# A hybrid decoder layer: first feed-forward pair without block sums, shared raw buffers, operands moved to multiples of 256 bytes

## The chip, the cores and the metric

The kernel runs on one core of one Trainium2 chip. The metric is the device time of one launch in microseconds (us); lower is better. Five engines matter: TensorE (PE, matrix products into PSUM; PEld is its weight load), VectorE (DVE), ScalarE (ACT), GpSimd (POOL) and SyncE (SP), which issues most of the loads. Each engine works off its own queue in a fixed order.

## The reference, cut to what matters

One decoder layer on 1024 tokens of width 1024: a mixer of sparse attention and retention, and then the feed-forward part, which is all that the change touches.

```python
h = h + mix @ w_out[l]                      # 1024 tokens x 1024
hn = rms_norm(h, ln2_w[l])                  # h * rsqrt(mean(h*h) + EPS) * weight
h = h + jnp.square(jax.nn.relu(hn @ w_up[l])) @ w_down[l]   # 1024 -> 4096 -> 1024
```

## The kernel before, in words

All matrices are float32. A product is made of float32r pieces: each operand is split into a rounded high part (a cast on ScalarE, line 1003) and the rest (a subtraction on VectorE, line 174), and high x high, high x low and low x high are added up: three matmuls of 128x128 weights by 512 columns for one block of products.

`h` lies transposed in the tiles `hac0` to `hac7`, 128 features each, 1024 tokens in two halves. When the last row of the output projection is added to a tile (line 945), `scaled` stores the sum to the DRAM tensor `dH` through the POOL queue and multiplies it by the norm's weight. The norm's factor itself is put on later, since relu squared commutes with a positive factor: `v2` and `r2` are made from the squares of `h` (function `scale`), and `add` applies them.

The up projection goes by 16 pairs of weight tiles (`NU`). A pair is a 2x2 block product (two weight tiles by two halves of features, two halves of tokens), done by a scheme that takes 7 block products instead of 8 and pays with sums: of the weights (`sums_up`: S1 to S4), of `h` (`early_sums`, `late_sums`: T1 to T4, made once) and of the results. A block product is 4 feature tiles x 3 matmuls = 12 matmuls, so a pair has 84. Products are named by their weight operand: 11, 12, S2, S1, S3, S4, 22. The bank `px` collects 11, then S2, S3 and 22 on top, and between two of them ScalarE copies an intermediate value out (lines 1114 and 1122), so the next product waits for that copy.

`fetch_up` loads a pair's weights in four tiles of 256 KB (`small`, four buffers), `first_up` splits 11 and 12, `rest_up` the five others, each into one of 12 operand slots: 8 are the former `hac` tiles, on the left side of the memory, 4 (`wo8` to `wo11`) lie in the pool `fw` on the right side. The pools on the right side start below the small constants, at a remainder of 224 bytes to the next multiple of 256; the left side is at multiples of 256. The results are relu'd, squared and stored to `dU` (line 1108).

`scale` runs after pair 6 and after pair 8, for half the tokens each: eight loads of `h` into the buffers `tmp`, which the intermediate results use too, eight squares on ScalarE, seven adds on VectorE, a product with ones and a reciprocal.

The down projection takes the 32 tiles of `dU` and of `w_down` in 8 groups of four, split into `fd` (and `ma`) tiles, through four raw buffers that are allocated when the up phase has released its pools. Each group has 192 matmuls.

The order on each engine is not the program's: a scheduler places the instructions by a timeline of its own, and the queues then keep that order. Pools hand out buffers by tags; a new tile waits until the buffer's last user is done.

Of the kernel before, what the change touches and what calls it, by code (L numbers as in the profile page):

```python
# [101 lines left out]
def hybrid_layer(ctx, tc, xT, x, wfm, wv, vecs, pe, w1, w2, w_out, w_up, w_down,  # L102
# [48 lines left out]
    r1 = cst.tile([128, NT], F32, name="r1")  # L151
# [798 lines left out]
    def early():  # L950
# [4 lines left out]
        r2.extend(hs.tile([128, 512], F32, name=f"r2{hf}") for hf in range(2))  # L955
# [36 lines left out]
    NU, NG, CH = 16, 8, 4  # L992
    ups = ExitStack()
# [18 lines left out]
    def small(nm):  # L1012
        return fw.tile([128, 512], F32, name=nm, tag="w" + nm[0], bufs=4)
# [10 lines left out]
    def early_sums(m):  # L1024
        t2 = op.tile([128, 512], F32, name=f"t2{m}", tag="t2", bufs=2)
        minus(quarter(0, m, 0), quarter(0, m, 1), quarter(0, m, 0))
        minus(t2, quarter(1, m, 1), quarter(0, m, 0))
        split(part("T2", m), t2)
        minus(quarter(1, m, 0), quarter(1, m, 0), t2)

    def late_sums():
        for m in range(4):
            split(part("T1", m), quarter(0, m, 0))
        yield
# [3 lines left out]
        yield  # L1038
        for m in range(4):
            split(part("22", m), quarter(1, m, 1))  # L1040
        yield
        for m in range(4):
            split(part("T4", m), quarter(1, m, 0))
        yield
# [3 lines left out]
    def operand(p, n):  # L1048

        i = next(slots)  # L1050
# [12 lines left out]
    def first_up(p):  # L1063
        wu[p] = {}
        for i, n in enumerate(("11", "12")):
            wu[p][n] = operand(p, n)
            split(wu[p][n], wr[p][i])

    def sums_up(p):

        a1, a2, b1, b2 = wr[p]
        s1, s2, s3, s4 = (small(f"s{p}{i}") for i in range(4))
        minus(s1, b1, b2, ALU.add)
        minus(s2, s1, a1)
        minus(s3, a1, b1)
        minus(s4, a2, s2)
        wr[p] = s2, s1, s3, s4, b2

    def rest_up(p):

        for n, t in zip(("S2", "S1", "S3", "S4", "22"), wr.pop(p)):
            wu[p][n] = operand(p, n)
            split(wu[p][n], t)
            yield
# [3 lines left out]
    def up(p):  # L1088
# [20 lines left out]

        x = px.tile([128, 512], F32, name=f"px{p}")  # L1110
# [26 lines left out]

    fetch_up(0)
# [4 lines left out]
    sums_up(0)  # L1143
    pacc = Ring("A4")

    def ready(o, hf):
        scaled(o, 1)
        if o >= 4:
            early_sums(o - 4)
# [6 lines left out]
    for n in ("T1", "T3", "22", "T4"):  # L1156
        hhi[n] = [hq.tile([128, 512], F32R, name=f"bh{n}{m}") for m in range(4)]
        hlo[n] = [hq.tile([128, 512], F32R, name=f"bl{n}{m}") for m in range(4)]

    v2 = {}  # L1160

    def scale(hf):

        for o in range(NK):
            h = fp.tile([128, 512], F32, name=f"hs{o}{hf}", tag="tmp", bufs=6)
            nc.sync.dma_start(h, dH[o][:, 512 * hf:512 * hf + 512])
            if o == 0:
                nc.scalar.activation(r2[hf], h, AF.Square)
            else:
                nc.scalar.activation(h, h, AF.Square)  # L1170
                nc.vector.tensor_tensor(r2[hf], r2[hf], h, op=ALU.add)
        ps = pz.tile([128, 512], F32, name=f"pr{hf}")
        nc.tensor.matmul(ps, ones, r2[hf], start=True, stop=True)
        v2[hf] = fp.tile([128, 512], F32, name=f"rv2{hf}", bufs=1)
        nc.vector.tensor_scalar(v2[hf], ps, scalar1=1.0 / D, scalar2=EPS, op0=ALU.mult, op1=ALU.add)
        nc.vector.reciprocal(r2[hf], v2[hf])

    fetch_up(1)
    first_up(1)
    first = [up(0), up(1)]  # L1180
    for u in first:
        next(u)
    for _ in alternate(rest_up(0), late_sums()):
        pass
    sums_up(1)
    for _ in rest_up(1):
        pass
    fetch_up(2)
    for _ in first[0]:
        pass  # L1190
    first_up(2)
    for _ in first[1]:
        pass
    for p in range(2, NU):
        sums_up(p)
        for _ in rest_up(p):
            pass
        if p + 1 < NU:
            fetch_up(p + 1)
# [168 lines left out]
```

## Time and profile before

| | us |
|---|---|
| median of 3 runs (lowest, highest) | 1359.34 (1353.59, 1360.81) |
| profiled execution, its own time | 1358.02 |
| its span, first to last instruction | 1356.3 |
| PE busy | 1289.7 (95%) |
| DVE, ACT busy | 834.5 (62%), 610.2 (45%) |
| mean granted TensorE clock | 0.982 of full speed |

A busy PE is not a PE at its peak: its matmuls overlap, so their lengths (0.39 us) add up to more than the time they take. What counts is the distance from one start to the next, about 0.23 us for 512 columns, and the idle times between. Where the granted clock falls to half, the distance is 0.43 us.

### The profile page before, as it was taken

Reading aid. Unit: us, or ns where it says so; the run is one execution under the profiler, and the core shown is the slowest. Engines: PE = TensorE matmul, PEld = TensorE weight load, DVE = VectorE, ACT = ScalarE, POOL = GpSimd, SP = SyncE. Lnnn points to the kernel's source line nnn. Section 1 sums busy time; section 2 is a strip of 40 time slices with the busy share of each in tenths; the row PEclk is TensorE's granted clock in tenths of the full one; section 3 lists DMA queues with packets and bytes.
Section 4 is the critical chain, followed back from the end, with each engine's and each line's share of the span. In section 5 each row is a group of like instructions: output and inputs, shape, how many; then the busy total and the mean of one; then the engine's idle time right before and its main releaser. Section 6 shows DMA issues by size and latency. Waiting matters only on the chain.

```text
span 1356.3 us, 19627 instructions
## 1 busy us (share of the span) xinstructions
PE 1289.7 (95%) x6862; PEld 1100.9 (81%) x6862; DVE 834.5 (62%) x1920; ACT 610.2 (45%) x1225; POOL 320.4 (24%) x464
## 2 busy tenths in 40 slices
PE   8999998999999998899699998899989999999998
PEld 6888877999999887778488776688768888888886
DVE  7695774777788974777973545644357255434522
ACT  7333314577787773455664545454444022201200
POOL 0453335455565661121000110010100000000013
PEclk9999999999999999899899998899989999999999
DMA  6567398122222517921243333332386033213102
GB/s 231 160 207 218 111 275 267 59 87 87 79 75 79 214 55 206 253 93 56 72 152 101 117 127 115 132 125 86 112 301 216 31 124 125 78 47 124 62 31 93
DMA packets 82770, 175.73 MB, mean 130 GB/s; under 512 B 10944, under 2 KB 27712, under 8 KB 82672
## 3 DMA queue, kind: packets, MB, share of 16 engines
q1 hardware_dynamic: 68256, 127.51, 31.4%
q0 software_dynamic: 14416, 46.97, 9.0%
q8 instruction: 54, 0.88, 0.3%
q14 instruction: 44, 0.36, 0.1%
HBM read 123.91 MB, written 50.46 MB: 129 GB/s over the span
## 4 chain that ended last, share of the span: by engine, by line
PE 38%; issue 17%; DMA 4%; POOL 2%; DVE 1%; ACT 1%; POOLq 0%; SPq 0%; ACTq 0%; DVEq 0%
PE pd L1229 9%; PE pd L1231 9%; PE pd L1230 9%; DMA rg<-dRG 2%; PE px L1097 2%; PE px L1099 2%; PE px L1098 2%; POOL dU L1108 1%; PE py L1099 1%; PE py L1097 1%; PE py L1098 1%; DMA dMix<-m 1%; DMA mixa<-dMix 0%; DMA dwr<-in_w_down 0%; PE pz L1097 0%
## 5 line engine op out<-in xcount | busy, mean ns | idle before, releaser
L1229 PE MATMUL pd<-du,dw 128*128 128x512 f32 x512 | 198.4, 393 | 5.6 <-ACT dw L1003 5.6
L1230 PE MATMUL pd<-du,dw 128*128 128x512 f32 x512 | 199.3, 389 | 0.0
L1231 PE MATMUL pd<-du,dw 128*128 128x512 f32 x512 | 198.8, 389 | 0.0
L1238 DVE TENSOR_TENSOR y<-pd,y 128x512 f32<-128x512 f32 x128 | 87.4, 689 | 167.3 <-PE pd L1231 167.3
L1003 ACT CAST du<-dur 128x1024 fp32r<-128x1024 f32 x32 | 33.7, 1052 | 199.9 <-PE pd L1230 175.2
L1229 PEld LDWEIGHTS pd<-du,dw 128*128 128x128 f32 x512 | 97.1, 190 | 26.2 <-ACT dw L1003 6.0
L1230 PEld LDWEIGHTS pd<-du,dw 128*128 128x128 f32 x512 | 96.2, 188 | 20.2
L1231 PEld LDWEIGHTS pd<-du,dw 128*128 128x128 f32 x512 | 96.2, 188 | 19.9
L1108 POOL DMA_DIRECT2D dU<-u x64 | 34.7, 542 | 312.7 <-ACT u L1107 312.7
L1240 POOL TENSOR_TENSOR y<-y,r 128x512 f32<-128x512 f32 x14 | 18.1, 1295 | 331.9 <-DVE y L1238 331.9
L174 DVE TENSOR_TENSOR tl<-pt,th 128x512 fp32r<-128x512 f32 (+2 forms) x136 | 80.1, 597 | 14.7 <-ACT th L783 14.0
L783 ACT CAST th<-pt 128x512 fp32r<-128x512 f32 (+2 forms) x136 | 68.1, 515 | 22.5 <-PE pt L838 20.1
L1097 PE MATMUL px<-bhT,wS 128*128 128x512 f32 x128 | 55.1, 430 | 20.7 <-ACT s L1114 12.3
L838 PE MATMUL pt<-ident,p 128*128 128x128 f32 x456 | 71.8, 275 | 0.8 <-DVE sbias L706 0.5
L830 PE MATMUL po<-tl,v 128*128 128x256 f32 (+1 forms) x272 | 70.2, 293 | 0.8 <-DVE tl L174 0.8
L830 PE MATMUL po<-th,v 128*128 128x256 f32 (+1 forms) x272 | 68.7, 274 | 0.1
L774 POOL TENSOR_SCALAR p<-p,rs 128x896 f32<-128x896 f32 (+3 forms) x64 | 47.8, 747 | 48.3 <-DVE rs L772 20.4
L174 DVE TENSOR_TENSOR w<-raw,w 128x512 fp32r<-128x512 f32 x48 | 32.9, 690 | 40.0 <-ACT w L1003 39.1
L838 PEld LDWEIGHTS pt<-ident,p 128*128 128x128 f32 x456 | 52.4, 141 | 5.0 <-DVE tl L174 1.4
L1003 ACT CAST wS<-s 128x512 fp32r<-128x512 f32 x64 | 39.6, 618 | 36.9 <-PE px L1099 22.4
L758 ACT ACTIVATE p<-p,mn 128x896 f32<-128x896 f32 (+3 forms) x64 | 49.8, 778 | 13.7 <-DVE mn L751 13.0
L830 PEld LDWEIGHTS po<-tl,v 128*128 128x128 f32 x272 | 51.6, 190 | 2.1 <-DVE tl L174 1.4
(426 smaller groups left out, 3726.5 us busy)
## 6 DMA issues: line engine op xcount, KB each, us to landing
raw<-in_w_up SPq DMA_DIRECT2D x64, 256.0 KB, 3.1
dU<-u POOLq DMA_DIRECT2D x64, 256.0 KB, 2.7
dur<-dU SPq DMA_DIRECT2D x32, 512.0 KB, 4.6
dwr<-in_w_down SPq DMA_DIRECT2D x32, 512.0 KB, 4.6
xraw<-in_xT SPq DMA_DIRECT2D x16, 256.0 KB, 5.4
w1r<-in_w SPq DMA_DIRECT2D x32, 128.0 KB, 3.6
dQ<-stg_Q POOLq DMA_DIRECT2D x8, 512.0 KB, 5.3
q<-dQ SPq DMA_DIRECT2D x64, 64.0 KB, 2.4
```

Source lines behind the costliest of these rows:

```text
L174: eng.tensor_tensor(lo, src, hi.bitcast(F32), op=ALU.subtract)
L758: nc.scalar.activation(buf[:, :n], buf[:, :n], AF.Exp, scale=-1.0, bias=mn[:, u, fin:fin + 1], accum_out=sm[:, 0, u, 0:1])
L783: nc.scalar.copy(th[:, :w], pt[:, :w])
L830: mm = nc.tensor.matmul(po[:, cs], vals[g, kt // 4][:, kt % 4, br], q[:, o:o + 128 * len(us)], start=False, stop=end and q is parts[1])
L838: nc.tensor.transpose(pt[:, o:o + 128], res[u][0][:, c:c + 128], ident)
L1003: nc.scalar.copy(to[0], raw)
L1097: nc.tensor.matmul(ps, wh[:, cs], bh, start=first and m == 0, stop=False, skip_group_check=not first)
L1108: nc.gpsimd.dma_start(dU[2 * p + i][:, 512 * hf:512 * hf + 512], u)
L1229: nc.tensor.matmul(ps, wh[:, cs], uh[:, ts], start=i == 0, stop=False)
L1230: nc.tensor.matmul(ps, wl[:, cs], uh[:, ts], start=False, stop=False)
L1231: nc.tensor.matmul(ps, wh[:, cs], ul[:, ts], start=False, stop=i == CH - 1)
L1238: nc.vector.tensor_tensor(y, ps, y, op=ALU.add)
```

## The change

- Pair 0 is computed as the plain 2x2 product: 8 block products, no sums of weights or results. Its `h` operands 12 and 22 are split as soon as `h` is ready; the sums T1 to T4 of `h` are formed after it and first used by pair 1. T3 takes the buffers of 12.
- All raw loads, of the weights up, of `h` for the squares and of both down operands, go through one pool `raws` of three buffers of 512 KB, which stays for both phases. `sums_up` forms its sums in place, in the raw tiles.
- The squares of `h` are taken over whole tiles, one tile after each pair from 4 on (`norm`), instead of eight half tiles at once after pairs 6 and 8.
- The last pair uses only the 8 left slots, and the `fd` tiles are laid out so that the first group's lie where buffers become free first.
- `r1` is padded by 56 floats, which moves every right-side pool to a multiple of 256 bytes.

```diff
-    r1 = cst.tile([128, NT], F32, name="r1")
+    r1 = cst.tile([128, NT + 56], F32, name="r1")[:, :NT]
@@
-        r2.extend(hs.tile([128, 512], F32, name=f"r2{hf}") for hf in range(2))
+        r2.append(hs.tile([128, S], F32, name="r2"))
@@
+    raws = ctx.enter_context(tc.tile_pool(name="raws", side="right", reuse_waits="tile", bufs=3))
@@
-    def small(nm):
-        return fw.tile([128, 512], F32, name=nm, tag="w" + nm[0], bufs=4)
+    def raw_tile(nm):
+        return raws.tile([128, S], F32, name=nm, tag="raw")
@@ operand
-        i = next(slots)
+        i = next(j for j in slots if j < 8 or p < NU - 1)
@@ fetch_up
-            wr[p] = [small(f"raw{p}{i}") for i in range(4)]
+            wr[p] = [raw_tile(f"raw{p}{i}") for i in range(2)]
             for i, t in enumerate(wr[p]):
-                nc.sync.dma_start(t, w_up[2 * p + i // 2][:, 4 * (i % 2):4 * (i % 2) + 4].rearrange("p k c -> p (k c)"))
+                nc.sync.dma_start(t, w_up[2 * p + i].rearrange("p k c -> p (k c)"))
@@ sums_up
+        a1, a2, b1, b2 = blocks(p)
+        s1 = fw.tile([128, 512], F32, name=f"s{p}", tag="s", bufs=2)
+        minus(s1, b1, b2, ALU.add)
+        minus(b1, a1, b1)
+        minus(a1, s1, a1)
+        minus(a2, a2, a1)
+        del wr[p]
+        for n, t in (("S2", a1), ("S1", s1), ("S3", b1), ("S4", a2), ("22", b2)):
+            wu[p][n] = operand(p, n)
+            split(wu[p][n], t)
@@ up
+        if p == 0:
+            for hf, pair in ((0, ("11", "21")), (1, ("12", "22"))):
+                for i, ring in enumerate((px, py_)):
+                    ps = ring.tile([128, 512], F32, name=f"pp{hf}{i}")
+                    for j in range(2):
+                        product(ps, f"{i + 1}{j + 1}", pair[j], j == 0)
+                    relu2(ps, i, hf)
+                yield
+            return
@@ ready
-        if o >= 4:
-            early_sums(o - 4)
+        split(part("22" if o >= 4 else "12", o % 4), quarter(o // 4, o % 4, 1))
@@
-    def scale(hf):
+    def norm():
         for o in range(NK):
-            h = fp.tile([128, 512], F32, name=f"hs{o}{hf}", tag="tmp", bufs=6)
-            nc.sync.dma_start(h, dH[o][:, 512 * hf:512 * hf + 512])
+            h = raw_tile(f"hs{o}")
+            nc.sync.dma_start(h, dH[o])
...
+            yield
@@
+    for _ in up(0):
+        pass
+    fetch_up(1)
+    first_up(1)
+    for m in range(4):
+        early_sums(m)
+    both(hr, "T3", "12")
+    late_sums()
+    sums = norm()
+    for p in range(1, NU):
+        fetch_up(p + 1)
+        sums_up(p)
+        for _ in up(p):
+            pass
+        first_up(p + 1)
+        if p >= 4:
+            next(sums, None)
@@ down
+            pool, tag = (ma, f"m{2 * i + j}") if odd and n == 3 else (fd, f"d{odd}{n}{i}{j}")
+        firsts = [(0, 2, *x) for x in ij]
+        homes = {k: home(*k) for k in [(g, n, *x) for g, n in ((1, 0), (1, 1), (1, 2), (0, 3)) for x in ij]
+                 + firsts[:2] + [(0, n, *x) for n in (0, 1) for x in ij] + firsts[2:]}
@@
-                    raw = fd.tile([128, S], F32, name=f"d{nm}r{f}", tag="raw", bufs=4)
+                    raw = raw_tile(f"d{nm}r{f}")
```

Up to the start of the feed-forward part the order on every engine stays as it was. Three places behind it follow; the numbers at the names are buffer numbers.

VectorE where pair 0 begins, before: `s00` to `s03` are sums of weights, `t20` and `t21` parts of T2, `w11_0` is the low part of the first operand.

```order
L174 TENSOR_TENSOR w11_0_8462<-raw00_8422,w11_0_8462 128x512
L174 TENSOR_TENSOR w12_0_8465<-raw01_8423,w12_0_8465 128x512
L945 TENSOR_TENSOR hac3_6135<-ob311_8572,hac3_6135 128x512
L1007 TENSOR_TENSOR s01_8469<-s00_8468,raw00_8422 128x512
L1007 TENSOR_TENSOR s02_8470<-raw00_8422,raw02_8424 128x512
L1007 TENSOR_TENSOR hac0_6008<-hac0_6008 128x512
L945 TENSOR_TENSOR hac7_6243<-ob711_8585,hac7_6243 128x512
L1007 TENSOR_TENSOR hac1_6055<-hac1_6055 128x512
L1007 TENSOR_TENSOR hac2_6098<-hac2_6098 128x512
L1007 TENSOR_TENSOR s03_8471<-raw01_8423,s01_8469 128x512
L1007 TENSOR_TENSOR t20_8502<-hac4_6160,hac0_6008 128x512
```

The same place now: all four weight operands of pair 0, and then `bl12`, `bl22` (low parts of the `h` operands 12 and 22) among the first differences for T1.

```order
L175 TENSOR_TENSOR w11_0_8479<-raw00_8443,w11_0_8479 128x512
L175 TENSOR_TENSOR w12_0_8482<-raw00_8443,w12_0_8482 128x512
L175 TENSOR_TENSOR w21_0_8485<-raw01_8444,w21_0_8485 128x512
L175 TENSOR_TENSOR w22_0_8488<-raw01_8444,w22_0_8488 128x512
L946 TENSOR_TENSOR hac3_6134<-ob311_8581,hac3_6134 128x512
L1009 TENSOR_TENSOR hac0_6007<-hac0_6007 128x512
L175 TENSOR_TENSOR bl120_8431<-hac0_6007,bh120_8427 128x512
L946 TENSOR_TENSOR hac7_6242<-ob711_8596,hac7_6242 128x512
L175 TENSOR_TENSOR bl220_8439<-hac4_6159,bh220_8435 128x512
L1009 TENSOR_TENSOR hac1_6054<-hac1_6054 128x512
L175 TENSOR_TENSOR bl121_8432<-hac1_6054,bh121_8428 128x512
```

The sums of weights are gone from this place, and what only pair 1 needs stands behind what pair 0 needs.

ScalarE in the middle of the up phase, before: `hs` are tiles of `h` for the squares, `s17` is the copy that product S2 of pair 7 waits for.

```order
L1107 ACTIVATE u106_9711<-u106_9711 128x512
L1168 ACTIVATE r20_6000<-hs00_9715 128x512
L1170 ACTIVATE hs10_9718<-hs10_9718 128x512
L1003 CAST wS4_9_10102<-s93_10088 128x512
L1170 ACTIVATE hs20_9722<-hs20_9722 128x512
L1170 ACTIVATE hs30_9726<-hs30_9726 128x512
L1170 ACTIVATE hs40_9730<-hs40_9730 128x512
L1114 COPY s17_9802<-px7_9788 128x512
L1170 ACTIVATE hs50_9734<-hs50_9734 128x512
```

ScalarE at the corresponding place now, one tile of `h` in a pair's round: `s27` is the copy that product S3 of pair 7 waits for, `raw90` and `raw100` are weights of pairs 9 and 10.

```order
L1120 COPY s17_9722<-px7_9708 128x512
L1005 CAST wS3_8_9845<-raw81_9685 128x512
L1104 ACTIVATE u106_9670<-u106_9670 128x512
L1103 ACTIVATE u007_9737<-s17_9722 128x512
L1104 ACTIVATE u007_9737<-u007_9737 128x512
L1181 ACTIVATE hs4_9972<-hs4_9972 128x1024
L1128 COPY s27_9754<-px7_9708 128x512
L1131 COPY s57_9768<-py7_9741 128x512
L1005 CAST w11_9_9966<-raw90_9830 128x512
L1005 CAST wS4_9_9994<-raw90_9830 128x512
L1005 CAST w12_10_10115<-raw100_9976 128x512
L1005 CAST wS2_9_9985<-raw90_9830 128x512
```

The copy `s17` now stands ahead of the square, and `s27` right behind it.

ScalarE at the passage from the up to the down phase now (before, the order was the same but for the last square, which stood ahead of the first cast): `u1015` is the last result of the up phase, `d0000` and `d0010` the first operands of the down phase.

```order
L1103 ACTIVATE u0115_10962<-s215_10916 128x512
L1104 ACTIVATE u0115_10962<-u0115_10962 128x512
L1103 ACTIVATE u1015_10978<-px15_10870 128x512
L1005 CAST d0000_11007<-dur0_11017 128x1024
L1005 CAST d0010_11009<-dwr0_11021 128x1024
L1005 CAST d0100_11011<-dur1_11025 128x1024
L1104 ACTIVATE u1015_10978<-u1015_10978 128x512
L1005 CAST d0110_11013<-dwr1_11029 128x1024
```

The first casts of the down phase stand behind the relu of the last bank of the up phase.

## Rows read from the trace of the kernel before

**Rows 1.** Windows: busy us (count) of PE, PEld, DVE, ACT, POOL; clock; DMA.

```profile
641.90:708.50 66.60, 54.44 (x215) 42.25 (x214) 57.54 (x96) 41.98 (x74) 6.72 (x13) 0.92 0.33 114
708.50:995.10 286.60, 273.42 (x1145) 217.92 (x1144) 137.62 (x202) 143.72 (x254) 30.08 (x56) 0.98 0.36 118
...
1000.60:1350.80 350.20, 350.16 (x1536) 289.55 (x1536) 160.38 (x193) 63.31 (x62) 18.13 (x14) 0.99 0.31 106
```

**Rows 2.** Waits of PE from 590 us on: total us, times, longest.

```profile
PE px L1097 <- ACT s L1114: 12.3, 4, 5.0
PE px L1097 <- ACT s L1122: 8.4, 4, 6.3
PE pd L1229 <- ACT dw L1003: 5.6, 1, 5.6
```

**Rows 3.** Timeline, PE: start, us, line, tiles, [idle before, releaser].

```profile
645.80 0.50 PE L1099 MATMUL px<-bh,w 128*128 128x512 f32 x1 [0.68 <-DVE w L174]
...
675.82 0.80 PE L1097 MATMUL px<-bhT,wS 128*128 128x512 f32 x1 [6.34 <-ACT s L1122]
...
817.54 0.80 PE L1097 MATMUL px<-bhT,wS 128*128 128x512 f32 x1 [4.90 <-ACT s L1114]
...
818.13 0.63 PE L1098 MATMUL px<-blT,wS 128*128 128x512 f32 x1
...
818.56 0.63 PE L1099 MATMUL px<-bhT,wS 128*128 128x512 f32 x1
...
1000.64 3.78 PE L1229 MATMUL pd<-du,dw 128*128 128x512 f32 x8 [5.59 <-ACT dw L1003]
1004.22 0.52 PE L1230 MATMUL pd<-du,dw 128*128 128x512 f32 x1
```

**Rows 4.** Timeline, VectorE and ScalarE where they work without a pause.

```profile
645.07 1.28 DVE L174 TENSOR_TENSOR w<-raw,w 128x512 fp32r<-128x512 f32 x2
...
667.76 2.19 ACT L1003 CAST bh<-hac 128x512 fp32r<-128x512 f32 x4
```

**Rows 5.** Timeline, PE: the 204th matmul of the up phase.

```profile
708.55 0.40 PE L1099 MATMUL px<-bhT,w 128*128 128x512 f32 x1
```

**Rows 6.** Timeline, ScalarE: the first square of the first `scale`.

```profile
812.90 0.63 ACT L1168 ACTIVATE r<-hs 128x512 f32<-128x512 f32 x1 [1.62 <-DMA hs<-dH]
```

**Rows 7.** Timeline, PE: first of 12 matmuls, first behind them; pairs 2, 3, down.

```profile
724.98 0.39 PE L1097 MATMUL py<-bh,wS 128*128 128x512 f32 x1
...
727.70 0.39 PE L1097 MATMUL px<-bh,w 128*128 128x512 f32 x1
...
744.64 0.40 PE L1097 MATMUL py<-bh,wS 128*128 128x512 f32 x1
...
747.44 0.40 PE L1097 MATMUL px<-bh,w 128*128 128x512 f32 x1
...
1100.48 0.39 PE L1229 MATMUL pd<-du,dw 128*128 128x512 f32 x1
...
1103.20 0.39 PE L1229 MATMUL pd<-du,dw 128*128 128x512 f32 x1
```

**Rows 8.** DMA issues: queue, count, KB each, median us to landing.

```profile
raw<-in_w_up SPq DMA_DIRECT2D x64, 256.0 KB, 3.1
...
dur<-dU SPq DMA_DIRECT2D x32, 512.0 KB, 4.6
...
rv<-dRV SPq DMA_DIRECT2D x8, 512.0 KB, 6.3
```

**Rows 9.** The tile `y`, loads of `dH` of 512 KB, window 940 to 990 us.

```profile
DMA to landing us min/median/max: 3.4/3.6/4.2
```

**Rows 10.** Groups, VectorE: add of 1024 elements; busy us, mean ns.

```profile
L236 DVE TENSOR_TENSOR xacc<-xacc,xsq 128x1024 f32<-128x1024 f32 x7 | 8.5, 1218 | 0.2 <-ACT xsq L234 0.2
```

**Rows 11.** Timeline, ScalarE at the passage to the down phase.

```profile
995.48 0.58 ACT L1106 ACTIVATE u<-px 128x512 f32<-128x512 f32 x1
...
999.55 1.04 ACT L1003 CAST dw<-dwr 128x1024 fp32r<-128x1024 f32 x1 [0.76 <-DMA dwr<-in_w_down]
```

More of the change, by code (lines that the diff above doesn't have):

```diff
@@ L1024, in early_sums @@
     def early_sums(m):
-        t2 = op.tile([128, 512], F32, name=f"t2{m}", tag="t2", bufs=2)
+        t2 = fw.tile([128, 512], F32, name=f"t2{m}", tag="s", bufs=2)
         minus(quarter(0, m, 0), quarter(0, m, 1), quarter(0, m, 0))
@@ L1136, in up, with both @@
         yield
+    hr = ups.enter_context(tc.tile_pool(name="hr", side="right", reuse_waits="tile", bufs=1))
+    def both(pool, n, tag):
+        hhi[n] = [pool.tile([128, 512], F32R, name=f"bh{n}{m}", tag=f"h{tag}{m}") for m in range(4)]
+        hlo[n] = [pool.tile([128, 512], F32R, name=f"bl{n}{m}", tag=f"l{tag}{m}") for m in range(4)]
+    for n in ("12", "22"):
+        both(hr, n, n)
     fetch_up(0)
@@ L1155, in hybrid_layer @@
     hq = ups.enter_context(tc.tile_pool(name="hq", side="right", reuse_waits="tile", bufs=1))
-    for n in ("T1", "T3", "22", "T4"):
-        hhi[n] = [hq.tile([128, 512], F32R, name=f"bh{n}{m}") for m in range(4)]
-        hlo[n] = [hq.tile([128, 512], F32R, name=f"bl{n}{m}") for m in range(4)]
+    for n in ("T1", "T4"):
+        both(hq, n, n)
     v2 = {}
-    def scale(hf):
+    def norm():
         for o in range(NK):
-            h = fp.tile([128, 512], F32, name=f"hs{o}{hf}", tag="tmp", bufs=6)
-            nc.sync.dma_start(h, dH[o][:, 512 * hf:512 * hf + 512])
+            h = raw_tile(f"hs{o}")
+            nc.sync.dma_start(h, dH[o])
@@ L1167, in scale @@
             if o == 0:
-                nc.scalar.activation(r2[hf], h, AF.Square)
+                nc.scalar.activation(r2[0], h, AF.Square)
             else:
                 nc.scalar.activation(h, h, AF.Square)
[L1171 to L1175, printed above, removed]
@@ L1176, in scale @@
-        nc.vector.reciprocal(r2[hf], v2[hf])
+                nc.vector.tensor_tensor(r2[0], r2[0], h, op=ALU.add)
+            yield
+        for hf in range(2):
+            r = r2[0][:, 512 * hf:512 * hf + 512]
+            ps = pz.tile([128, 512], F32, name=f"pr{hf}")
+            nc.tensor.matmul(ps, ones, r, start=True, stop=True)
+            v2[hf] = fp.tile([128, 512], F32, name=f"rv2{hf}", bufs=1)
+            nc.vector.tensor_scalar(v2[hf], ps, scalar1=1.0 / D, scalar2=EPS, op0=ALU.mult, op1=ALU.add)
+            nc.vector.reciprocal(r, v2[hf])
+            yield
@@ L1178, in hybrid_layer @@
+    for _ in up(0):
+        pass
     fetch_up(1)
     first_up(1)
[L1180 to L1194, printed above, removed]
-        sums_up(p)
[L1196 to L1199, printed above, removed]
-            first_up(p + 1)
+    for m in range(4):
+        early_sums(m)
@@ L1209, in hybrid_layer, with home @@
         pd = Ring("D8")
-        places = [[(fd, f"d{g}{i}") for i in range(12 + 4 * g)] + [(ma, f"m{k}") for k in range(4 - 4 * g)] for g in range(2)]
+        def home(g, n, i, j):
+            odd = g % 2
+            pool, tag = (ma, f"m{2 * i + j}") if odd and n == 3 else (fd, f"d{odd}{n}{i}{j}")
+            return pool.tile([128, S], F32R, name=f"d{g}{n}{i}{j}", tag=tag)
+        ij = list(itertools.product(range(2), range(2)))
+        firsts = [(0, 2, *x) for x in ij]
+        homes = {k: home(*k) for k in [(g, n, *x) for g, n in ((1, 0), (1, 1), (1, 2), (0, 3)) for x in ij]
+                 + firsts[:2] + [(0, n, *x) for n in (0, 1) for x in ij] + firsts[2:]}
         def load_down(g):
@@ L1219, in load_down @@
                     for j in range(2):
-                        pool, tag = places[(g + 1) % 2][4 * n + 2 * i + j]
-                        to.append(pool.tile([128, S], F32R, name=f"d{nm}{j}{f}", tag=tag))
+                        to.append(homes.get((g, n, i, j)) or home(g, n, i, j))
                     split(to, raw)
@@ L1239, in add @@
             if g == NG - 1:
[L1240 removed]
+                (nc.vector if o == NK - 1 else nc.gpsimd).tensor_tensor(y, y, r2[0][:, ts], op=ALU.mult)
                 nc.sync.dma_start(out[o][:, ts], y)
```

30 lines of the change are left out of this document (6 added, 24 removed).

## The prediction, made before the changed kernel ran

> **What bounds the kernel now.** I read the windows by stage first, then the waits of PE, then PE's timeline at each wait, and only then the other engines there. The windows [rows 1] show the feed-forward part in three stretches. In each the reader sees PE near the full span and VectorE and ScalarE well below it from 708 us on, so PE sets the time. What isn't PE at its peak is of three kinds: idle time (286.60 − 273.42 = 13.2 us in the second stretch), time at half clock (a mean of 0.98 over 286.6 us: 0.02 × 286.6 = 5.7 us lost) and matmuls that start too far apart (273.4 − 5.7 = 267.7 us for 1145 matmuls, 0.234 us each, where the down phase shows 2.72 us for 12, 0.2267 each [rows 7]). The waits of PE [rows 2] name ScalarE's copies out of `px` for 12.3 + 8.4 us and the casts at the passage to the down phase for 5.6. The timeline [rows 3] puts them at places: 6.34 us ahead of 675.82, 4.90 ahead of 817.54, 5.59 ahead of 1000.64. In the first stretch VectorE is busy 57.5 of 66.6 us: there PE runs ahead of VectorE, which has the sums of `h` to form beside the low parts.
>
> All terms below are against the profiled execution's span of 1356.3 us. Its own time is 1358.02; the median, 1359.34, is 1.3 above that.
>
> **Start of the up phase: −15.3 us.** Before, the 204th matmul starts at 708.55 [rows 5]. The third starts at 645.80, after a wait of 0.68 for the low part of `w11_0` [rows 3]. On VectorE one sum of weights that stood ahead is gone, an instruction of 0.60 us (two took 1.28 with their ends [rows 4]), so it starts at 645.2. Now the first 204 are 96 of pair 0, 72 of pair 1 and 36 of pair 2. Without waits the last would start at 645.2 + 201 × 0.2267 = 690.8. Three waits remain. `bl121` is the 39th VectorE instruction behind the last rows of the projection; at 0.60 each it ends about 1.2 us after PE asks for it. Casts on ScalarE take 0.52 each, (2.19 − 0.62) / 3 [rows 4]; one cast of weights stands behind a result: 0.5. Pair 2's first sums need the third raw buffer's load, about 0.8. Sum 2.5, so 693.3, and 708.55 − 693.3 = 15.3. T1 to T4 aren't late, because four products (48 matmuls, 10.9 us) now run between pair 0's end and the first use of a T. If that cover fails, VectorE's old delay returns: that is a rival below.
>
> **Pair 0 without sums: +2.7.** 96 instead of 84 matmuls, 12 × 0.2267. Its sums cost no PE time, and their time on VectorE is in the term above.
>
> **Addresses: −5.0.** Product S4 of pair 2 has weights and `h` both at a remainder of 224 bytes: 2.72 us for 12. S4 of pair 3 has weights in a left slot at remainder 0, `h` at 224: 2.80. Down, all at 0: 2.72 [rows 7]. So it is the mixture that costs 0.08 per product. 8 of 12 slots are left ones, and 1140 / 12 = 95 products are left at the 204th matmul: 0.08 × 2/3 × 95 = 5.1; I take 5.0. Bounds: nothing, if something else makes that 0.08, and 267.7 − 1145 × 0.2267 = 8.1, all that the second stretch has above its floor. The down rows exclude a loss.
>
> The Trainium skill speaks against this term: "SBUF — State Buffer", section "Who interferes with whom", gives PE two read ports, one for the moving operand and one for the weight load, independent of each other, so where the two lie relative to each other should not matter. The two S4 products differ by 0.08 us all the same, and by that page the sum would lack this term.
>
> **`scale` taken apart: −15.6.** Both calls put eight squares on ScalarE ahead of the copy that PE waits for: 4.90 us [rows 3] and, the longest of the four on line 1114, 5.0 [rows 2], 9.9 together. The first square itself waits 1.62 for its load [rows 6]. After such a stall PE shows half clock: starts 0.43 apart at 818.13 and 818.56 [rows 3], and the 5.7 us lost to the clock in this stretch stand behind these two stalls. Both go, since `s17` now stands ahead of the square. What is late next is the copy `s27`, directly behind a square of 1.04 us (a ScalarE operation of 1024 elements [rows 11]); I count 0.5 for it in the next term.
>
> **The norm by pairs: +2.5, between 0 and +21.** In pairs 4 to 11 three loads of 512 KB share three buffers: the tile of `h`, then two of weights, each waiting for the one before to be used. One round is: load, square 1.05, add 1.22 [rows 10], load, four casts of 0.52 = 2.1, load, five VectorE operations of 0.60 and a cast of 0.5 = 3.5. That is 7.9 + 3 L. PE needs 84 × 0.2267 = 19.05 per pair, so the chain binds from L = 3.72 on. Nearest in size are the `y` loads, 3.4 / 3.6 / 4.2 [rows 9]; `dur`, as large, took 4.6, and 256 KB of weights 3.1 [rows 8]. L = 3.6 costs nothing (18.7), 4.6 gives 21.7, so 2.65 × 8 rounds = 21. I take 3.8, next to the `y` loads since they too come one by one from a busy SP queue: 19.3, 0.25 × 8 = 2.0, and 0.5 for `s27`. Behind the waiting load on SP are the next weights, and behind those PE.
>
> The Trainium skill, "DMA: Bandwidth & Descriptors", section "Anatomy of one DMA — SWDGE (gpsimd) path", gives about 2.0 us plus the bytes by 436 GB/s, an estimate of 3.2 us for 512 KB; by that a round would be 17.5 us and the chain would never bind. It describes the POOL path, and the rows here are all longer.
>
> **Passage to the down phase: −2.5.** Before: 5.59 us idle, then eight matmuls from 1000.64 to 1004.22 [rows 3], 0.447 each, 8 × 0.22 = 1.8 lost: 7.4. Now the last bank's relu starts some 0.45 us after the bank's end, as at 995.48 [rows 11], takes 0.58, and two casts of 1.04 follow, with 0.3 between the engines: 3.4. The second step's weights come through the raw buffer after that, 0.5; the clock may still fall, 0 to 1.8, and I take 1.0. 4.9 instead of 7.4.
>
> The down phase itself (1536 matmuls, 350.2 us) I leave alone: a group of 192 takes 43.5 us, and its eight loads go through three buffers, three in 4.6 for the load, 1.04 for the cast and 1.2 for the low part, 6.9 us, so all in 19. SP's queue has nothing else to do there.
>
> Sum: −15.3 + 2.7 − 5.0 − 15.6 + 2.5 − 2.5 = −33.2. The span becomes 1323.1, the execution 1324.8, and set against the median 1326.
>
> **Rivals.** A measurement of this kernel can tell about 0.5% (6.8 us) from no change.
>
> The raw buffers bind: L is that of `dur`, 4.6. For it: three loads in a row wait for each other, and stores of `dU` run beside them. Against: 0.36 of the DMA time is used [rows 1]. 1326 − 2.5 + 21 = 1345.
>
> The addresses bring nothing: 1326 + 5.0 = 1331. For it, the rule above; against, [rows 7].
>
> The start is not won: VectorE forms T1 to T4 too late for pair 1, PE stalls there and drops to half clock as ahead of 675.82. For it: 57.5 of 66.6 us busy. Against: the sums of weights are gone from that place, and 48 matmuls cover it. It would give back about the 6.3 us of the old stall and as much again at half clock: 1326 + 12 = 1338.
>
> Slower: the loads in the rounds take as long as `rv`, 6.3 us for the same 512 KB [rows 8]. A round is then 7.9 + 18.9 = 26.8, 7.75 above PE's, 62 us in eight rounds: 1326 − 2.5 + 62 = 1385. It decides from L = 5.2 on (8 × (7.9 + 3 L − 19.05) = 35.7, all of the gain). Against: `rv` are eight loads that come at once, here at most three are under way. Between L = 4.9 and 5.5 it would be no change.
>
> The change does what it says: the order on ScalarE and VectorE shows the sums gone and the squares apart.
>
> **How the numbers follow.** Forecast 0.60 (its own range 1316 to 1334: all 8.1 of the addresses and no chain cost below, no dip avoided and 0.45 more per round above); addresses nothing 0.09; start not won 0.09; raw buffers bind 0.14; L near 5.2 0.04; slower 0.04. Faster by over 0.5% is the first four, 0.92; within 0.04; slower 0.04. The range 1316 to 1346 leaves out the last two and a tenth at its lower and upper ends.
>
> **What would show it.** Right: the 204th matmul near 693; 12 matmuls in 2.72 us with any slot; no idle time of over 2 us on PE between 700 and 960, and a clock of 1.0 there; loads of `hs` and of raw weights under 3.8 us; about 3.4 us idle at the passage. Wrong: PE waiting once a round for a copy behind a square or for weights of S1 that came late, in pairs 4 to 11; 2.80 us products left; a wait over 3 us where T1 to T4 are first used; a new wait in the first down group.

## The result and the profile after

The changed kernel takes 1321.7 us (median of four runs, 1320.74 to 1328.82) against 1359.4: a ratio of 0.974, 95% interval 0.970 to 0.979. The prediction, 1326 us and faster, was right, and its sum came within 3 us of the profiled execution: the span is 1320.1 us where 1323.1 had been worked out.

The windows of the changed kernel, with the columns and the three stretches of [rows 1] (from the first up matmul to the 204th, on to the last, the down phase):

```profile
640.60:691.00 50.40, 49.59 (x215) 39.66 (x214) 48.87 (x82) 36.73 (x66) 6.41 (x12) 1.00 0.35 123
691.00:961.80 270.80, 266.01 (x1157) 215.85 (x1155) 141.68 (x203) 144.11 (x251) 30.39 (x57) 1.00 0.41 135
964.70:1316.90 352.20, 348.83 (x1536) 288.22 (x1536) 162.41 (x196) 64.70 (x64) 18.68 (x15) 1.00 0.32 104
```

The granted clock is 1.00 in each, where it was 0.92, 0.98 and 0.99. VectorE is even fuller in the first stretch than before (48.9 of 50.4 us; 57.5 of 66.6), but PE hardly waits for it. The waits of PE in the feed-forward part, which answer to [rows 2]:

```profile
PE px L1094 <- ACT s L1128: 3.5, 5, 1.3
PE pd L1243 <- ACT d L1005: 3.0, 1, 3.0
...
PE px L1094 <- ACT s L1120: 1.2, 1, 1.2
PE pd L1243 <- DVE y L1252: 1.2, 1, 1.2
...
PE pp L1095 <- DVE bl L175: 0.5, 1, 0.5
```

The two copies out of `px` cost 4.7 us in all instead of 20.7, and no single wait but the passage is longer than 1.3. PE's timeline at the places of [rows 3, 5], with the first up matmul ahead:

```profile
640.70 0.39 PE L1094 MATMUL pp<-bh,w 128*128 128x512 f32 x1
...
658.94 0.50 PE L1095 MATMUL pp<-bl,w 128*128 128x512 f32 x1 [0.45 <-DVE bl L175]
...
666.33 0.50 PE L1094 MATMUL pz<-bh,w 128*128 128x512 f32 x1 [0.29 <-ACT w L1005]
...
690.78 0.39 PE L1096 MATMUL py<-bhT,wS 128*128 128x512 f32 x1
...
765.68 0.50 PE L1094 MATMUL px<-bhT,wS 128*128 128x512 f32 x1 [0.70 <-ACT s L1128]
...
880.86 0.50 PE L1094 MATMUL px<-bhT,wS 128*128 128x512 f32 x1 [1.26 <-ACT s L1128]
...
961.38 0.39 PE L1096 MATMUL px<-bhT,w 128*128 128x512 f32 x1
964.78 1.21 PE L1243 MATMUL pd<-d,d 128*128 128x512 f32 x4 [3.00 <-ACT d L1005]
...
988.02 0.50 PE L1243 MATMUL pd<-d,d 128*128 128x512 f32 x1 [1.15 <-DVE y L1252]
```

The 204th matmul is at 690.78, the last up matmul at 961.38, and the passage takes 3.39 us from start to start. Product S4 of pair 3, in a left slot, now takes 732.04 − 729.32 = 2.72 us, where [rows 7] had 2.80:

```profile
729.32 0.39 PE L1094 MATMUL py<-bh,wS 128*128 128x512 f32 x1
...
732.04 0.39 PE L1094 MATMUL px<-bh,w 128*128 128x512 f32 x1
```

Where the 36.2 us of span came from, by the starts of four matmuls in each trace (before: first up matmul 641.99, 204th 708.32, last 994.66, first down 1000.64):

| stretch | before | after | difference | forecast |
|---|---|---|---|---|
| ahead of the up phase | 641.99 | 640.70 | −1.3 | none |
| first to 204th | 66.33 | 50.08 | −16.2 | −15.3 |
| 204th to last (12 more) | 286.34 | 270.60 | −15.7 | −15.4 |
| last to first down | 5.98 | 3.39 | −2.6 | −2.5 with the clock behind it |
| down phase to the end | 355.66 | 355.32 | −0.3 | |

### The profile page after: what moved, and what is told of

Its sections match the earlier page's. It is cut to its first block, busy times and chain, and to the rows that moved or that the text cites. A ratio compares the mean times of both kernels' runs of the same rounds, so it can differ in the third digit from the quotient of the medians.

```text
span 1320.1 us, 19505 instructions
## 1 busy us (share of the span) xinstructions
PE 1276.0 (97%) x6874; PEld 1093.2 (83%) x6874; DVE 828.9 (63%) x1907; ACT 606.7 (46%) x1215; POOL 320.4 (24%) x464
## 4 chain that ended last, share of the span: by engine, by line
PE 75%; DMA 8%; DVE 6%; issue 6%; ACT 3%; POOL 1%; SPq 1%; POOLq 0%; ACTq 0%; DVEq 0%
PE pd L1243 8%; PE pd L1244 8%; PE pd L1245 8%; PE px L1094 4%; PE po L831 4%; PE px L1095 4%; PE px L1096 4%; PE pt L839 3%; PE ss L718 2%; PE py L1096 2%; PE py L1095 2%; PE py L1094 2%; PE sw L718 1%; DMA ry<-dRK 1%; PE cps L424 1%
## 5 line engine op out<-in xcount | busy, mean ns | idle before, releaser
L1243 PE MATMUL pd<-d,d 128*128 128x512 f32 x512 | 195.9, 390 | 4.2 <-ACT d L1005 3.0
L1244 PE MATMUL pd<-d,d 128*128 128x512 f32 x512 | 199.2, 389 | 0.0
L1245 PE MATMUL pd<-d,d 128*128 128x512 f32 x512 | 199.0, 389 | 0.0
L1243 PEld LDWEIGHTS pd<-d,d 128*128 128x128 f32 x512 | 96.0, 188 | 25.0 <-ACT d L1005 3.4
L1005 ACT CAST d<-dur 128x1024 fp32r<-128x1024 f32 x32 | 33.7, 1052 | 174.9 <-PE pd L1244 147.7
L1245 PEld LDWEIGHTS pd<-d,d 128*128 128x128 f32 x512 | 96.1, 188 | 19.9
L1244 PEld LDWEIGHTS pd<-d,d 128*128 128x128 f32 x512 | 96.1, 188 | 19.8
L759 ACT ACTIVATE p<-p,mn 128x896 f32<-128x896 f32 (+3 forms) x64 | 49.8, 778 | 13.7 <-DVE mn L752 13.1
L1094 PE MATMUL px<-bhT,wS 128*128 128x512 f32 x120 | 48.1, 400 | 4.8 <-ACT s L1128 3.5
L831 PEld LDWEIGHTS po<-th,v 128*128 128x128 f32 x272 | 51.6, 190 | 1.0 <-ACT th L784 0.3
L1005 ACT CAST d<-dwr 128x1024 fp32r<-128x1024 f32 x32 | 33.7, 1053 | 37.3 <-DMA dwr<-in_w_down 25.8
```

Source lines behind the costliest of these rows:

```text
L831: mm = nc.tensor.matmul(po[:, cs], vals[g, kt // 4][:, kt % 4, br], q[:, o:o + 128 * len(us)], start=False, stop=end and q is parts[1])
L1005: nc.scalar.copy(to[0], raw)
L1094: nc.tensor.matmul(ps, wh[:, cs], bh, start=first and m == 0, stop=False, skip_group_check=not first)
L1243: nc.tensor.matmul(ps, wh[:, cs], uh[:, ts], start=i == 0, stop=False)
L1244: nc.tensor.matmul(ps, wl[:, cs], uh[:, ts], start=False, stop=False)
L1245: nc.tensor.matmul(ps, wh[:, cs], ul[:, ts], start=False, stop=i == CH - 1)
```

## The experiments

**Is it the remainder of the addresses?** Three kernels leave the order on every engine exactly as it was in their parent and only move operands. The first is the kernel before with the padding alone:

```diff
-    r1 = cst.tile([128, NT], F32, name="r1")
+    r1 = cst.tile([128, NT + 56], F32, name="r1")[:, :NT]
```

> The kernel before with the 56 floats of padding and nothing else: every engine's order is that of before, and all operands of the up and down products lie at multiples of 256 bytes. Theory (a mixture of remainders costs 0.08 us per product): every product of 12 matmuls takes 2.72 us, some 0.0044 us less per up matmul on average, 1344 x 0.0044 = 5.9 us, and perhaps 1.3 us ahead of the feed-forward part: about 1352, ratio 0.995. The stalls of 6.3, 4.9 and 5.0 us stay. Rival (where the operands lie makes no difference): 1359, ratio 1.000, and products of 2.80 us stay.

Measured: 1350.0 us, ratio 0.994 (0.992 to 0.996). Its S4 of pair 3 takes 743.43 − 740.71 = 2.72 us. It isn't the only one: of the products that no wait interrupts, the 57 with weights in a left slot took 2.77 to 2.80 us before, and here all 82, in either kind of slot, take 2.72. The stalls stay:

```profile
740.71 0.39 PE L1097 MATMUL py<-bh,wS 128*128 128x512 f32 x1
...
743.43 0.39 PE L1097 MATMUL px<-bh,w 128*128 128x512 f32 x1
```

```profile
PE px L1097 <- ACT s L1114: 12.4, 4, 5.4
PE px L1097 <- ACT s L1122: 8.4, 5, 5.6
PE pd L1229 <- ACT dw L1003: 5.8, 1, 5.8
```

From the 204th to the last up matmul it takes 281.77 instead of 286.34 us: 4.6 us of the forecast 5.0. Another 3.5 us are won ahead of the up phase in this profile, where 1.3 had been expected (last section).

The second moves both sides to a remainder of 224 (the padding goes from `r1`, which shifts the right side, to `r2`, which shifts the left):

```diff
-    r1 = cst.tile([128, NT + 56], F32, name="r1")[:, :NT]
+    r1 = cst.tile([128, NT], F32, name="r1")
@@
-        r2.append(hs.tile([128, S], F32, name="r2"))
+        r2.append(hs.tile([128, S + 56], F32, name="r2")[:, :S])
```

> The changed kernel without the padding of r1, but with r2 longer by 56 floats, so that left and right pools both lie at a remainder of 224; the order on every engine is that of the changed kernel. Theory (what costs is that the two operands, or those of successive products, lie at different remainders): no difference to the changed kernel, 1322, 2.72 us for every 12 matmuls. Rival (what counts is that an operand lies at a multiple of 256 itself): 0.0066 us more for each of 1356 up and 1536 down matmuls, 19 us, 1341.

Measured: 1327.7 us (1327.4 to 1331.3). The products are as fast as at 0: 2.72 us for 12 in the down phase (below), and 269.59 us from the 204th to the last up matmul against 270.60. So a remainder of 224 as such costs PE nothing. The 6 us more, which neither theory has, lie ahead of the up phase, whose first matmul comes at 647.57 (last section).

```profile
1100.06 0.39 PE L1245 MATMUL pd<-d,d 128*128 128x512 f32 x1
...
1102.78 0.39 PE L1245 MATMUL pd<-d,d 128*128 128x512 f32 x1
```

The third mixes 0 with 128 (`NT + 24` in place of `NT + 56`).

> The changed kernel with 24 instead of 56 floats of padding: the right pools at a remainder of 128, the left at 0, 772 of the up matmuls with operands at two remainders; same order. Theory, if any mixture costs: 2.80 us for 12 mixed matmuls and 5 to 6 us more than the changed kernel, 1327 to 1328. Rival, if only remainders to 128 or to 64 bytes count: 2.72 us everywhere, 1322.

Measured: 1329.4 us. S4 of pair 3, weights at 0 and `h` at 128, takes 736.77 − 733.98 = 2.79 us, and the 204th to last 274.94 us, 4.3 more than at 0; most of the rest of its 7.7 us lies ahead of the up phase, which begins 3.7 us later. So two operands at different remainders to 256 cost 0.07 to 0.08 us per product, at 128 as at 224, and operands at equal ones don't.

```profile
733.98 0.40 PE L1094 MATMUL py<-bh,wS 128*128 128x512 f32 x1
...
736.77 0.39 PE L1094 MATMUL px<-bh,w 128*128 128x512 f32 x1
```

**What were the stalls of `scale` worth?** The changed kernel with the squares as before:

```diff
-    def norm():
+    def scale(hf):
...
-    sums = norm()
@@
-        if p >= 4:
-            next(sums, None)
+        if p in (6, 8):
+            scale(p // 2 - 3)
```

> The changed kernel, but the squares of h as before: eight half tiles at once after pair 6 and after pair 8, through the buffers of intermediate results. Theory: two stalls of about 5 us come back and behind each a half clock that costs about 2.9 us, while the 1 to 3 us that the tiles of h cost in the raw buffers go: 1322 + 15.6 - 2 = 1335. Rival (the stalls of before came from the crowding of weights and sums in the old buffers, not from the squares): at most 3 us more than the changed kernel, 1325, no idle time of PE over 2 us in pairs 6 to 10.

Measured: 1337.5 us, 15.8 more than the changed kernel. From the 204th to the last up matmul it takes 284.57 us, 14.0 more than with the squares apart (13.6 expected); the mean clock there is 0.98 again, and the waits for line 1120 are back:

```profile
PE px L1094 <- ACT s L1120: 9.4, 3, 4.5
PE px L1094 <- ACT s L1128: 4.3, 4, 2.3
```

So the rival, that the stalls came from crowded buffers and not from the squares, fell (at most 1325 expected).

**What is the plain pair 0 worth?** The changed kernel with pair 0 by sums:

```diff
@@ first_up
-        for n, t in zip(("11", "12") if p else ("11", "12", "21", "22"), blocks(p)):
+        for n, t in zip(("11", "12"), blocks(p)):
@@ up
-        if p == 0:
-            for hf, pair in ((0, ("11", "21")), (1, ("12", "22"))):
...
@@
-    for n in ("12", "22"):
+    for n in ("T3", "22"):
         both(hr, n, n)
@@ ready
-        split(part("22" if o >= 4 else "12", o % 4), quarter(o // 4, o % 4, 1))
+        if o >= 4:
+            early_sums(o - 4)
+            split(part("22", o % 4), quarter(1, o % 4, 1))
@@
-    for _ in up(0):
-        pass
...
-    for p in range(1, NU):
+    for p in range(NU):
```

> The changed kernel, but pair 0 by block sums as the others (84 matmuls, T1 to T4 formed ahead of it, as before the change); raw buffers, squares and addresses as changed. Theory (at the start VectorE was late with sums, and the plain pair 0 is what covers it): the waits at the start come back, some 14 us with the half clock behind them, less 12 x 0.227 = 2.7 for the matmuls: 1322 + 11 = 1333, a wait of several us where a product needs T2 or T1. Rival (it is the other order around it and the raw buffers that made the start short): the 12 matmuls are saved and at most 3 us of waits come: 1319 to 1323.

Measured: 1343.7 us, 22 more than the changed kernel, twice what was expected. The window from 645 to 672 us (columns as in [rows 1]), of this kernel and then of the changed one:

```profile
645.00:672.00 27.00, 11.80 (x36) 8.10 (x37) 27.00 (x46) 17.07 (x31) 1.72 (x4) 0.74 0.10 41
```

```profile
645.00:672.00 27.00, 26.26 (x115) 21.09 (x114) 27.00 (x46) 22.90 (x42) 3.25 (x6) 1.00 0.29 102
```

VectorE works without a pause in both, with 46 instructions in the same 27 us. With sums PE gets 36 matmuls in that time and a mean clock of 0.74; with the plain pair it gets 115. What the change at the start does is not less work on VectorE but other work for PE while VectorE catches up. The two profiles are 25.2 us apart (the run of this kernel that was profiled is the slowest of its four, 1347.1). Of these, 18.7 lie between the first and the 204th up matmul, 1.0 ahead of them, 1.7 from there to the last, although 12 matmuls fewer follow, and 3.6 in the down phase, where the first result is waited for 1.8 us and half clock stands behind that wait and behind the passage. The two long waits, 8.8 and 4.4 us, stand not where a product first needs T2 or T1, as the theory said, but at weights of pair 1 (by its count the product is the second into `pz`):

```profile
PE pz L1094 <- ACT w L1005: 8.8, 1, 8.8
PE pz L1096 <- DVE w L175: 4.4, 1, 4.4
```

Their cast stands behind the casts for the sums of `h` on ScalarE, and their low part, which ends the second wait, behind those sums on VectorE:

```profile
663.44 0.67 DVE L175 TENSOR_TENSOR w<-raw,w 128x512 fp32r<-128x512 f32 x1
```

Even with an earlier cast PE could have done no more than two of these 12 matmuls before that. The waits are longer than the longest of the kernel before (6.3). That kernel wove pairs 0 and 1 into each other and this one doesn't, which may be why the size was missed; no run tests it.

**Does the chain through three raw buffers bind?** Each tile of `h` was loaded twice, then three times, into the same buffer:

```diff
             nc.sync.dma_start(h, dH[o])
+            nc.sync.dma_start(h, dH[o])
```

The kernel with three loads has two such lines.

> The changed kernel, each tile of h for the squares loaded twice into the same raw buffer, one load after the other. Theory (three loads and their uses make a chain of 7.9 + 3 L per round that is just as long as PE's 19.05): a fourth load of 3.6 to 4.1 us makes a round 23 to 23.5 us, 8 x 4.2 = 33 us more: 1355. Rival (the chain has slack, the loads are hidden): at most 3 us more, 1325.

> The changed kernel, each tile of h for the squares loaded three times into the same raw buffer, one load after the other. Theory (the round through the raw buffers has slack of about one load, which the second load used up): the third costs its full 4 us in each of eight rounds: 1328 + 8 x 4 = 1360. Rival (the scheduler's order absorbs it, or the waits for PE in the round leave room for two loads): 1333 or less.

Measured: 1328.6 us with two loads, 1346.2 with three. From the 204th to the last up matmul: 270.60 with one, 275.03 with two, 293.70 with three. So the second load (3.8 us, as the loads landed there) costs 0.55 us a round and the third 2.3; with three PE waits 17.3 us for line 1120:

```profile
PE px L1094 <- ACT s L1120: 17.3, 9, 3.3
```

These are waits for the copy that product S2 needs (`s17` in pair 7), which stands there behind casts of weights that wait for their loads. The first theory, that the round has no slack, fell: it would have made the second load cost 4 us a round. The second, that one load uses the slack up, fell too (1360 expected), and so did its rival (1333 or less). In the eight rounds with three loads PE waits 0.9, 2.6, 0.9, 3.3, 0.7, 2.4, 2.5 and 2.9 us, 2.0 on average, for 3.8 + 3.5 = 7.3 us of loads that were added; by that the slack is an estimated 5 us. One reservation: the scheduler knows of the longer loads, and with two loads as with three it put the copy that product S3 needs (line 1128, `s27` in pair 7) ahead of the square in all eight rounds, so that a late square no longer holds PE up. With two loads, for instance:

```profile
799.17 0.59 ACT L1128 COPY s<-px 128x512 f32<-128x512 f32 x1 [0.79 <-PE px L1096]
...
805.18 1.06 ACT L1182 ACTIVATE hs<-hs 128x1024 f32<-128x1024 f32 x1 [4.42 <-DMA hs<-dH]
```

So the slack is that of the chain through the raw buffers to the next weights. Of the path from the load of `h` over the square to that copy, which the changed kernel has, these two runs say nothing.

Then the tiles of `h` were taken out of the raw buffers, in halves through the buffers of intermediate results:

```diff
-            h = raw_tile(f"hs{o}")
-            nc.sync.dma_start(h, dH[o])
+            for hf in range(2):
+                h = fp.tile([128, 512], F32, name=f"hs{o}{hf}", tag="tmp", bufs=6)
+                nc.sync.dma_start(h, dH[o][:, 512 * hf:512 * hf + 512])
...
```

> The changed kernel, the tiles of h for the squares in two halves through the buffers of intermediate results, one tile per pair as now, so that the raw buffers carry weights alone. Theory (the chain through the raw buffers costs 1 to 3 us): the waits of PE in pairs 4 to 11 fall from 3 us to 1 or less: 1320. Rival (what waits there is the copy behind a square on ScalarE, wherever the tile lies): no difference, 1322.

Measured: 1324.2 us, no difference. The place did what the theory said: from the 204th to the last up matmul it takes 268.14 instead of 270.60 us, and in pairs 4 to 10 every 84 matmuls take 19.04 us, where they took 19.10 to 20.08. In the total it was given back: in the first down group the wait for the first result to leave its bank is 2.5 us where it was 1.15, with half clock behind it, 2.9 us in all, and the up phase begins 2.5 us later in this profile.

```profile
PE pd L1245 <- ACT d L1005: 3.0, 1, 3.0
PE pd L1245 <- DVE y L1254: 2.5, 1, 2.5
```

**Why 3.4 us at the passage?** The casts of `d0000` and `d0010` stand behind the last results on ScalarE although their data had been loaded long before. Their buffers, too, are free early; but tiles are handed out in the program's order, and first came those that lie over T4, which the last product reads. The tiles keep their addresses, but from two pools, with the early ones first:

```diff
+        fa = s1.enter_context(tc.tile_pool(name="fa", reuse_waits="tile", bufs=1))
         fd = s1.enter_context(tc.tile_pool(name="fd", reuse_waits="tile", bufs=1))
@@ home
+            late = odd or n == 3 or (n == 2 and i == 0)
-            pool, tag = (ma, f"m{2 * i + j}") if odd and n == 3 else (fd, f"d{odd}{n}{i}{j}")
+            pool, tag = (ma, f"m{2 * i + j}") if odd and n == 3 else (fa if late else fd, f"d{odd}{n}{i}{j}")
@@
-        homes = {k: home(*k) for k in [(g, n, *x) for g, n in ((1, 0), (1, 1), (1, 2), (0, 3)) for x in ij]
-                 + firsts[:2] + [(0, n, *x) for n in (0, 1) for x in ij] + firsts[2:]}
+        homes = {k: home(*k) for k in [(0, n, *x) for n in (0, 1) for x in ij] + firsts[2:]
+                 + [(g, n, *x) for g, n in ((1, 0), (1, 1), (1, 2), (0, 3)) for x in ij] + firsts[:2]}
```

> The changed kernel, the down operands at the same addresses, but from two pools, so that those of the first two steps of group 0 are handed out first and not behind tiles that wait for the last product. Their casts then stand ahead of the last results of the up phase on ScalarE, and down matmuls stand ahead of the last up product on PE. Theory (the 3.4 us at the passage are casts that stand behind the last bank's relu in the queue): no idle time over 1 us at the passage, 3 us less, 1318.5. Rival (the operands or the raw loads aren't there any earlier, or the casts now delay the copies of pair 15): PE waits as long in pair 15, 1322.

Measured: 1317.1 us (1314.7 to 1325.8), ratio 0.968 (0.965 to 0.971). 18 down matmuls stand ahead of the last up product, the step from the last up matmul to the next is 0.23 us, and the first down group has no wait. Its profiled execution is the slowest of the six (1325.8) and shows what a late load does. One tile of `h` landed after 6.2 us (the longest of its eight; 4.4 is their median). ScalarE waited 5.43 us for it and PE 1.98 for the copy behind the square. In the changed kernel (764.10 and 765.68) it was 4.16 and 0.70: ScalarE waited 1.27 us longer here, and PE 1.27. A wait of 3.31 us at 888.1 is the other large one. Whether such loads explain the spread of the other five isn't shown. ScalarE, and then PE:

```profile
825.09 1.06 ACT L1181 ACTIVATE hs<-hs 128x1024 f32<-128x1024 f32 x1 [5.43 <-DMA hs<-dH]
826.06 0.57 ACT L1128 COPY s<-px 128x512 f32<-128x512 f32 x1
```

```profile
826.68 0.50 PE L1094 MATMUL px<-bhT,wS 128*128 128x512 f32 x1 [1.98 <-ACT s L1128]
```

With both edits, the homes first and the tiles of `h` in halves:

> The changed kernel with both edits: the first down operands handed out first, and the tiles of h in halves through the buffers of intermediate results. Theory (the two act in different places and add up): no idle time at the passage, and none behind a square in pairs 4 to 11: 1317 - 2.5 = 1314.5. Rival (what the halves save in pairs 4 to 11 is given back in the first down group, as when they were tried alone): 1317.

Measured: 1316.2 us (1314.5 to 1319.0), between the two expectations. Then the changed kernel and the one with both edits were run side by side:

> The changed kernel as it is, on the same chip and beside the same runs of before as the next one, so that the two can be compared. Every theory: 1321.7 as before, ratio 0.974 to before.

> The kernel with both edits (down operands handed out first, tiles of h in halves through the buffers of intermediate results), beside the changed kernel. Theory (3 us of idle time gone at the passage, the waits behind squares gone): 5 us less than the changed kernel, 1316 to 1317, ratio 0.969. Rival (the 5 us of the runs so far are a difference between chips): within 2 us of the changed kernel.

Measured: 1323.5 and 1317.1 us; ratios to before 0.9738 (0.9713 to 0.9764) and 0.9686 (0.9666 to 0.9706), intervals that don't touch. So the kernel with both edits is faster than the changed kernel, on one chip. From the first up matmul to the last down matmul the two profiles take 672.5 and 667.2 us, 5.3 less with both edits, while the up phase begins 2.1 us later there. Whether both edits are needed is open: the homes alone gave the same 1317. The waits in the feed-forward part with both edits:

```profile
PE px L1094 <- ACT s L1128: 3.3, 4, 1.3
PE px L1094 <- ACT s L1120: 1.2, 1, 1.2
PE pp L1095 <- DVE bl L175: 0.4, 1, 0.4
```

## Why the prediction was right

**Start: right, 0.9 us too small.** The three waits that were priced at 2.5 us came as 0.45 for a low part of the `h` operand 12, 0.29 for a cast of weights, and none for the third raw load; with the matmuls that start late behind them and a few smaller delays it is 2.0. Two counts were off: the row of [rows 5] is the 205th up matmul, the 204th is at 708.32, so the same working gives 15.0; and 645.80 is the fifth up matmul by its start, not the third, which made the sum 0.45 us too long. The reason stands on the test of pair 0: VectorE's backlog is there as ever, and pair 0's own matmuls and the four products behind it cover it.

**Pair 0's 12 matmuls** weren't measured apart; at 0.2267 us each they cost the 2.7 us.

**Addresses: right.** 1134 undisturbed steps behind the 204th matmul have a mean of 0.2270 us where they had 0.2314; 1134 × 0.0044 = 5.0. The test of the padding alone gives 4.6, and that with all at 224 shows that it is the mixture. The Trainium skill, "SBUF — State Buffer", section "Who interferes with whom", calls PE's two read ports independent and says nothing of addresses; the 2.79 us of the mixture with 128 against 2.72 says that where the two operands lie relative to each other does matter here, by 3%.

**`scale` and the norm: the net was right, one reason was not.** −15.6 + 2.5 = −13.1 was forecast, 14.0 was measured when the squares were put back at once. But the 2.5 was worked out from a round of 7.9 + 3 L that just fills PE's 19.05 us, and this step failed. The loads landed as supposed:

```profile
DMA to landing us min/median/max: 4.0/4.2/5.0
...
DMA to landing us min/median/max: 3.3/3.6/5.8
```

(`hs`, then raw weights, from 700 to 900 us; the mean of the three is the 3.8 that was taken, though `hs` is above it.) The formula gives 7.9 + 4.2 + 2 × 3.6 = 19.3, and the loads of `hs` do follow each other by 19.1 to 20.1 us. But a round that is paced by PE looks the same, and one and two more loads showed about 5 us of slack in that chain. What PE does lose there, 2.6 us over pairs 4 to 10, is the other part of the term, the copy behind the square, which had been given 0.5. The path is shorter than the round, and PE stands at both its ends. ScalarE waits for PE to finish product 22 of the pair before; the relu and the copy of line 1120 follow, then a cast from a raw buffer. VectorE's low part frees that buffer, SP issues the load of `h` into it, and the square and, behind it, the copy of line 1128 wait for the load (ScalarE, VectorE, SP, ScalarE):

```profile
756.63 0.60 ACT L1103 ACTIVATE u<-px 128x512 f32<-128x512 f32 x1 [0.37 <-PE px L1096]
...
757.59 0.63 ACT L1005 CAST wS<-raw 128x512 fp32r<-128x512 f32 x1
```

```profile
758.35 0.68 DVE L175 TENSOR_TENSOR wS<-raw,wS 128x512 fp32r<-128x512 f32 x1
```

```profile
759.05 0.33 SPq L1177 DMA_DIRECT2D hs<-dH  x1
```

```profile
764.10 1.06 ACT L1181 ACTIVATE hs<-hs 128x1024 f32<-128x1024 f32 x1 [4.16 <-DMA hs<-dH]
765.06 0.57 ACT L1128 COPY s<-px 128x512 f32<-128x512 f32 x1
```

PE's 0.70 us ahead of 765.68 end there. This path has no slack then: with the homes first, a load that kept ScalarE 1.27 us longer kept PE 1.27 us longer. So the rival of the raw buffers had the right place for a danger (a late load reaches PE) and the wrong way for it. PE's longest wait in that stretch, 1.26 us ahead of 880.86, is not behind a square: there the copy of line 1128 stands behind a cast that waits 3.28 us for its load of weights, and the wait is there with the tiles in halves too (1.47).

Two kernels that both load `h` in halves through the other buffers part the two terms: from the 204th to the last up matmul it takes 284.57 us with the squares at once and 268.14 with one tile a pair, 16.4 us where 15.6 had been worked out, and 2.46 less than the changed kernel's 270.60, where 2.5 had been. That the 2.5 came so close is luck: 2.0 of it was for a round that doesn't bind, and 0.5 for the copy that cost nearly all of it.

**Passage: right.** 3.4 us were worked out for the start of the down phase and 3.39 came. The half clock behind it, taken at 1.0, and the wait for the second step's weights, taken at 0.5, were none, and in their place came a wait of 1.15 us in the first down group that had not been forecast (988.02 above): the first result leaves its bank behind a low part on VectorE. In the second profile of the changed kernel the down phase begins 1.0 us later and this wait is 0.2, so time won ahead of it can be lost here. No run takes the shared raw buffers or the layout of the `fd` tiles back, so what each of them gives at the passage isn't shown.

**The rest of the difference.** 1.3 us are ahead of the up phase and in no term. And 1.3 us had been added since the median of before lay above its profiled execution; that of after doesn't (1321.7 and 1321.9). The lower end of the prediction's own range, 1316, doesn't follow from what it names: with 8.1 for the addresses and no cost of the chain the sum is 1320.4.

Of the signs of being wrong that the prediction names, two showed on a small scale: PE does wait for copies behind squares (0.06 to 1.04 us a round), and there is a new wait in the first down group. Loads of `hs` took 4.2 us where under 3.8 was the sign of being right.

Of the rivals, that of the addresses is refuted by the padding alone and by the tests at 128 and 224. That of the start didn't come: no wait there is longer than 0.45 us. That of loads of 6.3 us met single loads as long (6.2 and 6.1 in the profile with the homes first), but never as a median.

## What to carry to other kernels

A queue that can't keep up at the start of a stage needs no less work if the engine behind it has plain work to do meanwhile: here 12 more matmuls (2.7 us) took 18.7 us of waits and half clock off the start, by the test of pair 0. An operation that waits for a load shouldn't stand ahead of a copy that PE waits for, since PE can then be late by as much as the load is. A chain that comes out just as long as the bounding engine's round may only be following it; lengthen it by a known dose before believing that it binds, and look whether the order stayed the same when you did.

## What the runs showed of the hardware that was not expected

The time of a load may depend on the address that it goes to. Ahead of the up phase, where the order is the same in all these kernels and the DMA share is 0.88 to 0.98 (519 to 585 us, the three kernels below), the loads `rq` landed after these times (min, median, max; from 500 to 600 us). Changed kernel:

```profile
DMA to landing us min/median/max: 2.7/5.2/6.5
```

All at 224:

```profile
DMA to landing us min/median/max: 2.7/6.7/7.7
```

Before:

```profile
DMA to landing us min/median/max: 2.6/6.3/7.4
```

In the eleven profiles with operands at multiples of 256 the medians are 5.2 to 5.9 us. The two kernels with a side at 224 lie above them, the one with a side at 128 (5.8) among them. A stretch of some 320 matmuls there (515.2 to 581.7 us in the changed kernel) took 66.5 to 69.4 us in the eleven, and 70.0 (before), 69.7 (128) and 72.5 us (all at 224) in the others. It holds 2.6 of the 3.5 us that the padding alone won ahead of the up phase, and 6.0 of those that the kernel at 224 lost. But the two kinds lie close together, and the three kernels with `h` in halves, one tile a pair (68.3 to 69.4), which are at multiples of 256 too, are near the upper end. In the eleven, the up phase begins anywhere from 638.4 to 643.9 us, and before it was 641.99. The interval of the padding's ratio, 5 to 11 us, doesn't tell the 9 us measured from the 6 that the products explain either. So the address is a candidate and not shown to be the cause; a test with such loads alone was not made.
